# Where the up projection's four combinations of x are formed, and how many column pairs go the plain way

## The chip, the cores and the metric

The kernel runs on one core of a Trainium2 chip. The metric is the device time of one execution in microseconds (us). TensorE does the matmuls (PE in the profile, its weight loads PEld), VectorE is DVE, ScalarE is ACT, GpSimd is POOL, and SyncE (SP) issues most DMAs. All data is fp32; a matmul operand is split into a high and a low fp32r part ("hi" and "lo", hi + lo = the value), so that every product takes three matmuls.

## The reference, cut to what matters

One decoder layer: a hybrid mixer, a cross-attention, and the gated MLP below, with an RMSNorm around each. The change sits where the cross-attention's output becomes the MLP's input.

```
y = memory_cross_attention(rmsnorm(h, g[2]), rmsnorm(mem, mem_norm_g), w_q, w_kv, w_o)
h = h + rmsnorm(y, g[3])
x3 = rmsnorm(h, g[4])                              # (1024 tokens, 1024 columns)
u = causal_dwconv(x3 @ w_up, conv_w) + conv_b      # w_up: 1024 x 5632
a, b = split(u, 2)                                 # 2816 columns each
y = (silu(a) * b) @ w_down
```

## The kernel before, in words

**The cross-attention's output.** A loop over eight token tiles of 128 tokens, `t` = 0 to 7. In each, `token_mm` makes y for the tile in two PSUM banks (48 matmuls of 128x512), `post_norm` normalises it and adds the residual (L1005 to L1012), and L1103 to L1106 form `hr`, the normalised input of the MLP. Eight PE transposes of `hr` (L230, into two PSUM banks `tp_x3...`) and a split (ACT L232 writes hi, DVE L233 writes lo) make the transposed tile; it is put on the list `pend` and emitted behind the y of the next tile. Below, "token t" is this loop's tile, and `tp_x` of token t its transposes.

**x3** lies in SBUF as eight tiles [128, 4, 512]: token half (0 or 1) by part (hi, lo) by half of the 1024 columns. B11 and B21 are the two column halves of the first token half, B12 and B22 those of the second.

**The up projection** goes over 22 pairs of column blocks, `j` and `j + 22`. The first `PLAIN` pairs (three) go the plain way: for each block and token half 24 matmuls (`plain_mm`), so 96 a pair. The others go by `strassen_pair`, one level of the Strassen-Winograd scheme in seven half products of 12 matmuls, so 84 a pair. It needs the four combinations T1 = B12 - B11, T2 = B22 - T1, T3 = B22 - B12, T4 = B21 - T2, each as hi and lo tiles, and seven weight operands (A11, A12, A22, S1 to S4), which `up_operands` makes from the two raw weight blocks: four sums on POOL (L1151), seven splits on ACT (L1156) and DVE (L1157).

**The combinations** are made by `x_combinations`, in eight slices of 64 tokens: POOL adds hi and lo of the four B (L1198), DVE subtracts (L1201), ACT and DVE split the four results (L1203, L1204). Per slice 4 POOL, 8 DVE and 4 ACT instructions of 128x256. Four slices are written between the plain pairs 0 and 1, four behind pair 1.

**Order.** A scheduler fixes every engine's instruction order when the kernel is built; each engine then runs its own list in order. PSUM is split into tags: `mm` (5 banks) and `g` (3 banks) up to the end of the plain pairs, then `set_psum(b=8)` makes eight banks for the Strassen pairs, which come free when the old ones have been read out (`plain_out`, L1216). The pool `ap_` (`a_tile`) has nine buffers of 8 KB a partition (a tile of x3 or T, or the pair of tiles `ua`, fills one); the raw weight blocks have two buffers.

Of the kernel before, what the change touches and what calls it, by code (L numbers as in the profile page):

```python
# [7 lines left out]
F32 = mybir.dt.float32  # L8
F32R = mybir.dt.float32r
I32 = mybir.dt.int32  # L10
AF = mybir.ActivationFunctionType
ALU = mybir.AluOpType
# [4 lines left out]
P = 128  # L17
T = 1024
# [4 lines left out]
NC = 8  # L23
NFF = 22
# [38 lines left out]
    return [(n, int(e[len(n):])) for n, e in zip(names, text.split())]  # L63


PLAIN = 3


@with_exitstack
def hybrid_layer(  # L70
# [4 lines left out]
    nc = tc.nc  # L75
# [23 lines left out]
    h1_d = dram.tile([NC, P, D], F32, name="h1_d")  # L99
    h2_d = dram.tile([NC, P, D], F32, name="h2_d")  # L100
    mid_d = dram.tile([NFF, P, T], F32, name="mid_d")

    const = ctx.enter_context(pool("const"))
    wpool = ctx.enter_context(pool("wpool"))
# [13 lines left out]
    def psum(tag, name):  # L118
        p, tags = psum_pool[0]
        return p.tile([P, 512], F32, tag=tag, name=name, bufs=tags[tag])  # L120
# [69 lines left out]
        plan(f"wa{k}", a_d[k], gain=par[:, O_G2 + k:O_G2 + k + 1], where=(WX, W)[k // 4])  # L190
    for k in range(KT):
        plan(f"wv{k}", vw_d[k], where=(WX, W)[k // 4])
    for j in (0, NFF, 1, 1 + NFF, 2, 2 + NFF):
        plan(f"up{j}", w_up[j])

    def rsqrt(a, n, name):
# [25 lines left out]
        dve.tensor_scalar(a, ssq, 1.0 / d, EPS, op0=ALU.mult, op1=ALU.add)  # L222
        return rsqrt(a, n, name)

    def transpose_split(src, hi, lo, name):
        for q in range(2):
            tp = psum("g", f"tp_{name}_{q}")
            for i in range(4):
                k = 4 * q + i
                pe.transpose(out=tp[:, i * P:(i + 1) * P], in_=src[:, k * P:(k + 1) * P], identity=ident)  # L230
            v = tp.rearrange("p (k t) -> p k t", k=4)
            act.activation(hi(q), v, AF.Copy)  # L232
            dve.tensor_tensor(lo(q), v, hi(q), op=ALU.subtract)  # L233
# [752 lines left out]
    def a_tile(shape, name, dtype=F32R):  # L986
        return ap_.tile(shape, dtype, tag="a", name=name, bufs=9)
# [92 lines left out]
    for n in range(2):  # L1080
        g = wpool.tile([P, 512], F32, tag="st", name=f"g4{n}", bufs=2)
        sync.dma_start(out=g, in_=gains[4:5, HS[n]].to_broadcast([P, 512]))
        g4.append(g)
    x3 = [[[], []], [[], []]]
    for t in range(NC):
        hf = t // 4
        hr = wk(f"hr{t}")
        sync.dma_start(out=hr, in_=h1_d[t])
        if t == NC - 1:
            flush()  # L1090
        o = token_mm(pT[t], "wv", f"y{t}", t in ENDS)
        flush()
        if t % 4 == 0:
            for i in range(2):
                for q in range(2):
                    nm = f"x3_{hf}_{i}_{q}"
                    x3[hf][i].append(x8.tile([P, 4, 512], F32R, tag="x8", name=nm, bufs=4) if hf == 0
                                     else a_tile([P, 4, 512], nm))
        y = wk(f"h2{t}")
        post_norm(o, g3, y, hr, sqrt_r)  # L1100
        nc.scalar.dma_start(out=h2_d[t], in_=y)
        ss = small(1, "ss4")
        act.activation(hr, y, AF.Square, accum_out=ss)  # L1103
        r = sqrt_r(ss, 1, "r4")
        for n in range(2):
            dve.scalar_tensor_tensor(out=hr[:, HS[n]], in0=y[:, HS[n]], scalar=r, in1=g4[n],  # L1106
                                     op0=ALU.mult, op1=ALU.mult)
        s = slice((t % 4) * P, (t % 4 + 1) * P)
        pend.append(lambda hr=hr, hf=hf, s=s, t=t: transpose_split(
            hr, lambda k: x3[hf][0][k][:, :, s], lambda k: x3[hf][1][k][:, :, s], f"x3{t}"))  # L1110

# [50 lines left out]
            c = slice(k * P, (k + 1) * P)  # L1164
            mm3(o, w[0][:, c], w[1][:, c], xx[0][:, k], xx[1][:, k], start and k == 0, k == 3, not start)

    def strassen_pair(j, W_, ua, ub):
        b = [psum("b", f"st{j}_{n}") for n in range(4)]
        p1 = wpool.tile([P, 512], F32, tag="st", name=f"p{j}", bufs=2)
        u3 = gbp.tile([P, 512], F32, tag="gb", name=f"u3_{j}", bufs=1)  # L1170
        half_product(b[0], W_["A11"], X["B11"], True)
        act.activation(p1, b[0], AF.Copy)
        half_product(b[1], W_["S2"], X["T2"], True)
        dve.tensor_tensor(p1, b[1], p1, op=ALU.add)
        half_product(b[2], W_["S1"], X["T1"], True)
        dve.tensor_tensor(u3, b[2], p1, op=ALU.add)
        half_product(b[3], W_["S3"], X["T3"], True)
        dve.tensor_tensor(ub[:, 0, HS[1]], b[3], u3, op=ALU.add)
        half_product(b[0], W_["A12"], X["B21"], False)
        act.activation(ua[:, 0, HS[0]], b[0], AF.Copy)  # L1180
        half_product(b[2], W_["S4"], X["B22"], False)
        dve.tensor_tensor(ua[:, 0, HS[1]], b[2], p1, op=ALU.add)
        half_product(b[3], W_["A22"], X["T4"], False)
        dve.tensor_tensor(ub[:, 0, HS[0]], b[3], p1, op=ALU.add)
        a = conv3(j, ua)
        gate_mid(j, a, conv3(j + NFF, ub))

    X = {}

    def x_combinations(cs):  # L1190

        for c in cs:
            s = slice(c * 64, c * 64 + 64)
            xr = tp.tile([P, 4, 4, 64], F32, tag="tmp", name=f"xr{c}", bufs=2)
            raw = {}
            for i, n in enumerate(("B11", "B12", "B22", "B21")):
                raw[n] = xr[:, i]
                nc.gpsimd.tensor_tensor(raw[n], X[n][0][:, :, s], X[n][1][:, :, s], op=ALU.add)  # L1198
            for o, p, m in (("T1", "B12", "B11"), ("T3", "B22", "B12"), ("T2", "B22", "T1"), ("T4", "B21", "T2")):
                raw[o] = raw[{"T1": "B11", "T3": "B12", "T2": "B22", "T4": "B21"}[o]]  # L1200
                dve.tensor_tensor(raw[o], raw[p], raw[m], op=ALU.subtract)  # L1201
            for n in ("T2", "T1", "T3", "T4"):
                act.activation(X[n][0][:, :, s], raw[n], AF.Copy)  # L1203
                dve.tensor_tensor(X[n][1][:, :, s], raw[n], X[n][0][:, :, s], op=ALU.subtract)  # L1204

    def plain_mm(jj, i):
        os_[jj, i] = psum("mm", f"up{jj}_{i}")
        up_half(jj, os_[jj, i], i)
# [12 lines left out]
    for jj in (0, NFF, 1):  # L1221
# [2 lines left out]
    wx_es.close()  # L1224
    up_es = ExitStack()
    tp = up_es.enter_context(pool("tp"))
    tt = lambda n, i: (a_tile([P, 4, 512], f"xT{n}{i}") if n in (1, 2) else
                       tp.tile([P, 4, 512], F32R, tag="t", name=f"xT{n}{i}", bufs=4))
    for jj in (0, NFF):
        plain_mm(jj, 1)  # L1230
    plain_out(0)
    for n, (hf, q) in {"B11": (0, 0), "B21": (0, 1), "B12": (1, 0), "B22": (1, 1)}.items():
        X[n] = (x3[hf][0][q], x3[hf][1][q])
    X.update({f"T{n}": (tt(n, 0), tt(n, 1)) for n in (2, 1, 3, 4)})
    x_combinations(range(4))
    plain_mm(1, 1)
    for i in range(2):
        plain_mm(1 + NFF, i)
    plain_out(1)
    x_combinations(range(4, 8))  # L1240
    for jj in (2, 2 + NFF):
        for i in range(2):
            plain_mm(jj, i)
    plain_out(2)
    ops = {PLAIN: up_operands(PLAIN)}
    set_psum(b=8)
    for j in range(PLAIN, NFF):
        if j + 1 < NFF:
            ops[j + 1] = up_operands(j + 1)
        strassen_pair(j, ops.pop(j), a_tile([P, 2, T], f"ua{j}", F32),  # L1250
                      a_tile([P, 2, T], f"ua{j + NFF}", F32) if j % 2 else
                      tp.tile([P, 2, T], F32, tag="ua", name=f"ua{j + NFF}", bufs=1))
    up_es.close()
    ap_es.close()
    x8_es.close()
# [227 lines left out]
```

## Time and profile before

| what | us |
|---|---|
| median of 3 runs (lowest, highest) | 1495.16 (1494.82, 1496.19) |
| the profiled execution: its own time | 1496.32 |
| its span (first to last instruction) | 1494.5 |
| PE busy in the span | 1434.6 (96%) |
| DVE, ACT, POOL busy | 1161.3, 695.3, 169.5 |

A busy share is an average over stages. The row of granted clock (PEclk) is TensorE's clock as a share of full speed: 1.00 is 2.4 GHz, 0.50 is 1.2 GHz. Times below are counted from the start of the span. The DMA queues in the page are two hardware queues (issued by SP and by ACT) and two for instructions; no DMA of this kernel is issued by POOL.

### The profile page before, as it was taken

To read this page: it belongs to the slowest core of one execution; us is meant where nothing else is said; L and a number is where in the kernel's file an instruction comes from. 1 tells how busy PE (TensorE), PEld (TensorE's weight loads), DVE (VectorE), ACT (ScalarE), POOL (GpSimd) and SP (SyncE) were. 2 spreads that over 40 slices of the span, in tenths; PEclk is the share of its full clock that TensorE was granted. 3 is DMA by queue.
4 is the path that set the end of the run, shared out by engine and by line. 5 is a ranking of instruction groups with operands and counts; after the bars stand their busy time and mean duration, and the time that the engine had idled before them with its cause. 6 is when DMAs were issued, how large, how long until landed. Compare 5 with 4: busy or idle time off the path is not lost.

```text
span 1494.5 us, 19452 instructions
## 1 busy us (share of the span) xinstructions
PE 1434.6 (96%) x7099; PEld 1186.8 (79%) x7099; DVE 1161.3 (78%) x1993; ACT 695.3 (47%) x1326; POOL 169.5 (11%) x118
## 2 busy tenths in 40 slices
PE   6999999998999899999999989999999999999996
PEld 6878888887897778788788867888888887788875
DVE  6699999993567778743556777888888887869997
ACT  6526464633556545433434443444444444554442
POOL 0000000000000000000000643333333330000000
PEclk9999999999999999999999999999999999999998
DMA  7533233339756775400523112222222225985472
GB/s 243 166 96 100 71 109 82 106 103 290 218 173 206 240 225 184 141 29 0 169 100 123 46 43 71 77 78 85 85 85 79 77 85 203 319 301 197 140 254 107
DMA packets 118560, 205.74 MB, mean 138 GB/s; under 512 B 17184, under 2 KB 58816, under 8 KB 118464
## 3 DMA queue, kind: packets, MB, share of 16 engines
q1 hardware_dynamic: 95488, 155.99, 33.4%
q10 hardware_dynamic: 22976, 48.51, 8.7%
q8 instruction: 56, 0.92, 0.3%
q14 instruction: 40, 0.33, 0.1%
HBM read 153.58 MB, written 50.87 MB: 137 GB/s over the span
## 4 chain that ended last, share of the span: by engine, by line
PE 49%; DVE 6%; DMA 3%; issue 2%; ACT 2%; POOL 1%; DVEq 0%; SPq 0%; ACTq 0%; POOLq 0%
PE st L236 8%; PE st L238 8%; PE st L237 8%; PE M L237 3%; PE M L238 3%; PE M L236 3%; PE y L237 2%; PE y L238 2%; PE y L236 2%; PE sc L236 1%; PE sc L237 1%; PE sc L238 1%; PE wo L237 1%; PE wo L238 1%; PE wo L236 1%
## 5 line engine op out<-in xcount | busy, mean ns | idle before, releaser
L238 PE MATMUL pj<-xT,w_in 128*128 128x512 f32 x384 | 150.3, 391 | 1.2 <-DVE w_in L133 1.2
L352 DVE SCALAR_TENSOR_TENSOR ca<-sg,par,ca 128x1023 f32<-128x1023 f32 (+18 forms) x120 | 150.1, 1267 | 1.1
L236 PE MATMUL pj<-xT,w_in 128*128 128x512 f32 x384 | 150.8, 393 | 0.1
L237 PE MATMUL pj<-xT,w_in 128*128 128x512 f32 x384 | 149.9, 390 | 0.0
L237 PE MATMUL M<-wM 128*128 128x512 f32 x308 | 121.1, 393 | 4.6 <-DVE wM L1317 2.7
L1127 DVE SCALAR_TENSOR_TENSOR ua<-ua,par 128x1023 f32<-128x1023 f32 x88 | 115.6, 1315 | 9.7 <-ACT ua L1125 7.0
L236 PE MATMUL M<-wM 128*128 128x512 f32 x308 | 118.9, 392 | 4.4 <-ACT wM L132 3.5
L238 PE MATMUL M<-wM 128*128 128x512 f32 x308 | 120.8, 392 | 0.0
L236 PE MATMUL st<-xT,wst 128*128 128x512 f32 x304 | 118.7, 391 | 0.0
L238 PE MATMUL st<-xT,wst 128*128 128x512 f32 x304 | 118.4, 390 | 0.0
L237 PE MATMUL st<-xT,wst 128*128 128x512 f32 x304 | 118.2, 389 | 0.0
L236 PE MATMUL st<-x,wst 128*128 128x512 f32 x228 | 93.9, 412 | 9.2 <-ACT ua L1216 5.7
L1198 POOL TENSOR_TENSOR xr<-x,x 128x256 f32<-128x256 f32 x32 | 32.4, 1045 | 579.4 <-DVE hr L1106 562.2
L132 ACT ACTIVATE wM<-rbM 128x1024 fp32r<-128x1024 f32 x55 | 58.0, 1062 | 75.1 <-PE M L238 53.7
L238 PE MATMUL st<-x,wst 128*128 128x512 f32 x228 | 91.5, 401 | 0.0
L237 PE MATMUL st<-x,wst 128*128 128x512 f32 x228 | 91.3, 400 | 0.0
L1157 DVE TENSOR_TENSOR wst<-sums,wst 128x512 fp32r<-128x512 f32 x76 | 60.7, 818 | 35.0 <-ACT wst L1156 35.0
L1156 ACT ACTIVATE wst<-sums 128x512 fp32r<-128x512 f32 x76 | 43.8, 621 | 90.0 <-POOL sums L1151 90.0
L238 PEld LDWEIGHTS pj<-xT,w_in 128*128 128x128 f32 x384 | 72.1, 188 | 16.2 <-DVE w_in L133 1.5
L236 PEld LDWEIGHTS pj<-xT,w_in 128*128 128x128 f32 x384 | 72.1, 188 | 14.8 <-ACT w_in L132 0.3
L237 PEld LDWEIGHTS pj<-xT,w_in 128*128 128x128 f32 x384 | 72.2, 188 | 14.5
L133 DVE TENSOR_TENSOR wM<-rbM,wM 128x1024 fp32r<-128x1024 f32 x55 | 67.0, 1226 | 8.4 <-ACT wM L132 8.4
(376 smaller groups left out, 3654.7 us busy)
## 6 DMA issues: line engine op xcount, KB each, us to landing
rbM<-in_w_down SPq DMA_DIRECT2D x132, 256.0 KB, 4.0
raw_up<-in_w_up SPq DMA_DIRECT2D x44, 512.0 KB, 3.6
raw_in<-in_w_in SPq DMA_DIRECT2D x24, 512.0 KB, 3.7
mid_d<-ua ACTq DMA_DIRECT2D x22, 512.0 KB, 2.6
ma<-mid_d SPq DMA_DIRECT2D x44, 256.0 KB, 5.4
raw_kv<-in_w_kv SPq DMA_DIRECT2D x16, 512.0 KB, 4.4
h_d<-h ACTq DMA_DIRECT2D x16, 512.0 KB, 2.7
xr<-in_x ACTq DMA_DIRECT2D x8, 512.0 KB, 4.4
```

Source lines behind the costliest of these rows:

```text
L132: act.activation(w[:, 0], raw, AF.Copy)
L133: dve.tensor_tensor(w[:, 1], raw, w[:, 0], op=ALU.subtract)
L236: pe.matmul(o, lhsT=wh, rhs=xh, start=start, stop=False, skip_group_check=onto)
L237: pe.matmul(o, lhsT=wh, rhs=xl, start=False, stop=False, skip_group_check=onto)
L238: pe.matmul(o, lhsT=wl, rhs=xh, start=False, stop=stop, skip_group_check=onto)
L352: dve.scalar_tensor_tensor(out=ca[:, d:], in0=sg[:, :T - d], scalar=par[:, wb + 30 - d:wb + 31 - d], in1=ca[:, d:], op0=ALU.mult, op1=ALU.add)
L1127: dve.scalar_tensor_tensor(out=a[:, d:], in0=u[:, :T - d], scalar=fw(2 - d), in1=a[:, d:], op0=ALU.mult, op1=ALU.add)
L1156: act.activation(w[:, i, 0], op[s], AF.Copy)
L1157: dve.tensor_tensor(w[:, i, 1], op[s], w[:, i, 0], op=ALU.subtract)
L1198: nc.gpsimd.tensor_tensor(raw[n], X[n][0][:, :, s], X[n][1][:, :, s], op=ALU.add)
```

## The change

`x_combinations` goes, with its 32 POOL, 64 DVE and 32 ACT instructions. In its place `x3_tile` takes over the split of a transposed tile and, for tokens 4 to 7 (the second token half, when the first is there), also forms the four combinations of the tile's 128 tokens: B12 and B22 are read straight from the transposes' two PSUM banks, B11 and B21 as hi and lo from `x3`. That is six DVE subtractions or additions of 128x512 and one ACT copy a token. Those of tokens 4 to 6 are written by POOL to a DRAM tile `xt_d`, four DMAs of 256 KB a token in pieces of 512 bytes; those of token 7 stay in SBUF.

Later, between the plain pairs, `x_combination(i)` loads what tokens 4 to 6 left of one combination from `xt_d` into the place of its lo tile by a DMA of SP (768 KB in pieces of 1536 bytes), and ACT and DVE split it in two instructions each: 128x1536 for the loaded part, 128x512 for the part in SBUF. `PLAIN` is 2: pair 2 now goes by Strassen, with three banks of tag `g` and one of `mm` for its sums, before `set_psum(b=8)`. T3 and T4 take the buffers of `ap_` that T1 and T2 had.

```
-PLAIN = 3
+PLAIN = 2
...
+    xt_d = dram.tile([4, P, 4, 512], F32, name="xt_d")
...
-    for j in (0, NFF, 1, 1 + NFF, 2, 2 + NFF):
+    for j in (0, NFF, 1, 1 + NFF):
         plan(f"up{j}", w_up[j])
...
+    TN = (2, 1, 3, 4)
+    xt_last = []
+
+    def x3_tile(hr, hf, s, t):
+        tps = []
+        transpose_split(hr, lambda k: x3[hf][0][k][:, :, s], lambda k: x3[hf][1][k][:, :, s], f"x3{t}", tps)
+        if hf == 0:
+            return
+        xt = a_tile([P, 4, 512], f"xt{t}", F32)
+        v = [xt[:, i].rearrange("p (k t) -> p k t", k=4) for i in range(4)]
+        b12, b22 = (tp.rearrange("p (k t) -> p k t", k=4) for tp in tps)
+        sub = lambda o, a, b: dve.tensor_tensor(o, a, b, op=ALU.subtract)
+        act.activation(v[2], b12, AF.Copy)
+        sub(v[1], b12, x3[0][0][0][:, :, s])
+        sub(v[1], v[1], x3[0][1][0][:, :, s])
+        sub(v[0], b22, v[1])
+        sub(v[2], b22, v[2])
+        sub(v[3], x3[0][0][1][:, :, s], v[0])
+        dve.tensor_tensor(v[3], v[3], x3[0][1][1][:, :, s], op=ALU.add)
+        if t == NC - 1:
+            xt_last.extend(v)
+            return
+        for i in range(4):
+            nc.gpsimd.dma_start(out=xt_d[i][:, :, s], in_=v[i])
...
-        pend.append(lambda hr=hr, hf=hf, s=s, t=t: transpose_split(
-            hr, lambda k: x3[hf][0][k][:, :, s], lambda k: x3[hf][1][k][:, :, s], f"x3{t}"))
+        pend.append(lambda hr=hr, hf=hf, s=s, t=t: x3_tile(hr, hf, s, t))
...
-    def strassen_pair(j, W_, ua, ub):
-        b = [psum("b", f"st{j}_{n}") for n in range(4)]
+    def strassen_pair(j, W_, ua, ub, tags="bbbb"):
+        b = [psum({"m": "mm"}.get(tag, tag), f"st{j}_{n}") for n, tag in enumerate(tags)]
...
+    def x_combination(i):
+
+        hi, lo = X[f"T{TN[i]}"]
+        n = 3 * P
+        raw = lo[:, :, 0:n].bitcast(F32)
+        sync.dma_start(out=raw, in_=xt_d[i][:, :, 0:n])
+        for r, s in ((raw, slice(0, n)), (xt_last[i], slice(n, n + P))):
+            act.activation(hi[:, :, s], r, AF.Copy)
+            dve.tensor_tensor(lo[:, :, s], r, hi[:, :, s], op=ALU.subtract)
...
     for jj in (0, NFF):
         plain_mm(jj, 1)
+    x_combination(0)
     plain_out(0)
-    x_combinations(range(4))
+    x_combination(1)
     plain_mm(1, 1)
+    x_combination(2)
     for i in range(2):
         plain_mm(1 + NFF, i)
+    x_combination(3)
     plain_out(1)
-    x_combinations(range(4, 8))
-    for jj in (2, 2 + NFF):
-        for i in range(2):
-            plain_mm(jj, i)
-    plain_out(2)
```

**PE, between the y of token 6 and the y of token 7.** `y_1_7374` (before) and `y_1_7387` (after) are the last sums of token 6, `y_0_7483` and `y_0_7520` with `y_1_7521` those of token 7, `tp_x_0` and `tp_x_1` the transposes of token 5's `hr`. Before:

```order
L237 MATMUL y_1_7374<-w_wv_6787,pT_6653 128x512
L238 MATMUL y_1_7374<-w_wv_6787,pT_6653 128x512
L230 MATMUL tp_x_0_7423<-ident,hr_7275 128x128 x4
L230 MATMUL tp_x_1_7430<-ident,hr_7275 128x128 x4
L236 MATMUL y_0_7483<-w_wv_6752,pT_6838 128x512
```

With the change, the same transposes, eleven matmuls into token 7's y:

```order
L239 MATMUL y_1_7521<-w_wv_6758,pT_6839 128x512
L240 MATMUL y_1_7521<-w_wv_6758,pT_6839 128x512
L233 MATMUL tp_x_0_7436<-ident,hr_7276 128x128 x4
L241 MATMUL y_1_7521<-w_wv_6758,pT_6839 128x512
L233 MATMUL tp_x_1_7443<-ident,hr_7276 128x128 x4
L239 MATMUL y_0_7520<-w_wv_6763,pT_6839 128x512
```

They stand between two matmuls of one sum now; a late `hr` stops the y of token 7 there.

**DVE, behind the transposes of token 5.** `x_1_1_...` is the lo part of the transposed tile, `h_...` the residual of token 6, `xt_7450` the new tile of combinations. Before:

```order
L233 TENSOR_TENSOR x_1_1_0_7243<-tp_x_0_7423,x_1_0_0_7241 128x4x128
L233 TENSOR_TENSOR x_1_1_1_7244<-tp_x_1_7430,x_1_0_1_7242 128x4x128
L215 RECIPROCAL pn_y<-pn_y 128x1
L216 SCALAR_TENSOR_TENSOR pn_u<-pn_y,pn_a 128x1
L217 SCALAR_TENSOR_TENSOR pn_y<-pn_u,pn_y 128x1
L1010 SCALAR_TENSOR_TENSOR h_7437<-y_0_7373,pn_y,gb_6740 128x512
L1010 SCALAR_TENSOR_TENSOR h_7437<-y_1_7374,pn_y,gb_6740 128x512
L1012 TENSOR_TENSOR h_7437<-h_7437,hr_7371 128x1024
```

With the change:

```order
L236 TENSOR_TENSOR x_1_1_0_7244<-tp_x_0_7436,x_1_0_0_7242 128x4x128
L236 TENSOR_TENSOR x_1_1_1_7245<-tp_x_1_7443,x_1_0_1_7243 128x4x128
L1013 SCALAR_TENSOR_TENSOR h_7462<-y_1_7387,pn_y,gb_6741 128x512
L1101 TENSOR_TENSOR xt_7450<-tp_x_0_7436,x_0_0_0_6854 128x512
L1015 TENSOR_TENSOR h_7462<-h_7462,hr_7384 128x1024
L1101 TENSOR_TENSOR xt_7450<-xt_7450,x_0_1_0_6856 128x512
L1101 TENSOR_TENSOR xt_7450<-tp_x_1_7443,xt_7450 128x512 x2
L1101 TENSOR_TENSOR xt_7450<-x_0_0_1_6855,xt_7450 128x512
L134 TENSOR_TENSOR w_up_7603<-raw_up_7601,w_up_7603 128x1024
L1108 TENSOR_TENSOR xt_7450<-xt_7450,x_0_1_1_6857 128x512
L215 TENSOR_SCALAR r_a<-ss_7480 128x1
```

The six new instructions stand among those that lead to token 6's `hr` (its `r_a` is the last row), and ahead of them.

**POOL, its list from the last memset on.** `xt_...` are the tiles of tokens 4, 5 and 6, `sums_...` the weight sums of the first Strassen pair. Before, 32 additions `xr` stood here; with the change:

```order
L1113 DMA xt_d<-xt_7342 512x1x128 x4
L1113 DMA xt_d<-xt_7450 512x1x128 x4
L1113 DMA xt_d<-xt_7508 512x1x128 x4
L1180 ISA
L1180 TENSOR_TENSOR sums_0_7909<-raw_up_7907 128x512
L1180 TENSOR_TENSOR sums_1_7910<-raw_up_7905,raw_up_7907 128x512
L1180 TENSOR_TENSOR sums_0_7909<-sums_0_7909,raw_up_7905 128x512
L1180 TENSOR_TENSOR sums_1_7910<-raw_up_7905,sums_0_7909 128x512
```

The first pair's sums now stand behind twelve DMA issues in place of 32 additions.

## Rows read from the trace of the kernel before

**Rows 1.** The waits of PE in the whole span: times waited, longest.

```profile
PE st L236 <- ACT ua L1216: 5.7, 1, 5.7
PE st L236 <- DVE u L1176: 3.5, 1, 3.5
```

**Rows 2.** Stretches: length, busy us (instructions) of PE, PEld, DVE, ACT, POOL; granted clock; DMA.

```profile
798.35:810.10 11.75, 11.75 (x57) 9.86 (x56) 7.66 (x17) 5.95 (x12) 0.00 (x0) 1.00 0.25 89
810.10:828.90 18.80, 18.55 (x88) 14.89 (x88) 10.23 (x21) 6.57 (x14) 5.48 (x8) 1.00 0.41 132
828.90:878.80 49.90, 49.90 (x216) 40.38 (x216) 44.13 (x74) 25.22 (x48) 27.23 (x26) 1.00 0.12 40
878.80:884.51 5.71, 0.00 (x0) 0.00 (x0) 3.78 (x8) 3.26 (x8) 4.13 (x3) 0.78 0.07 28
884.51:888.91 4.40, 4.40 (x11) 3.46 (x11) 3.94 (x4) 3.23 (x5) 2.87 (x2) 0.51 0.16 22
904.07:909.34 5.27, 5.27 (x12) 4.12 (x13) 1.89 (x3) 0.00 (x0) 0.00 (x0) 0.50 0.01 3
912.09:931.53 19.44, 19.44 (x85) 15.69 (x84) 15.83 (x18) 8.51 (x12) 7.18 (x4) 1.00 0.24 80
```

**Rows 3.** Timeline of POOL and ACT about 880 us: start, length, instruction, [idle before].

```profile
878.46 2.71 POOL L1151 TENSOR_TENSOR sums<-raw_up 128x512 f32<-128x512 f32 x1 [5.51 <-DVE xT L1204]
...
883.40 1.06 ACT L1216 ACTIVATE ua<-up 128x512 f32<-128x512 f32 x2
```

**Rows 4.** DVE by line, 828.9 to 878.8 us: busy, mean ns, idle before.

```profile
L1201 DVE TENSOR_TENSOR xr<-xr 128x256 f32<-128x256 f32 x30 | 17.0, 578 | 5.8 <-POOL xr L1198 5.3
L1127 DVE SCALAR_TENSOR_TENSOR ua<-ua,par 128x1023 f32<-128x1023 f32 (+1 forms) x8 | 12.1, 1514 | 0.0
L1204 DVE TENSOR_TENSOR xT<-xr,xT 128x256 fp32r<-128x256 f32 x29 | 11.4, 438 | 0.0
```

**Rows 5.** Timeline of DVE behind the y of token 5.

```profile
787.29 0.16 DVE L1007 TENSOR_TENSOR pn_s<-pn_ss 128x1 f32<-128x1 f32 x1 [2.32 <-ACT h L1005]
...
789.50 1.41 DVE L1010 SCALAR_TENSOR_TENSOR h<-y,pn_y,gb 128x512 f32<-128x512 f32 x2
790.95 1.22 DVE L1012 TENSOR_TENSOR h<-h,hr 128x1024 f32<-128x1024 f32 x1
...
795.22 1.42 DVE L1106 SCALAR_TENSOR_TENSOR hr<-h,r_y,g 128x512 f32<-128x512 f32 x2
```

**Rows 6.** The instructions on the transposes' banks, 700 to 830 us: shortest/median/longest ns.

```profile
L233 DVE TENSOR_TENSOR x<-tp_x,x x16: 680/691/692, 744.1 to 829.5; 128x512 fp32r<-128x512 f32 x16
```

**Rows 7.** Timeline of PE at the transposes of token 7.

```profile
827.61 1.04 PE L230 MATMUL tp_x<-ident,hr 128*128 128x128 f32 x8
828.90 0.98 PE L236 MATMUL up<-x,w_up 128*128 128x512 f32 x3 [0.25 <-ACT x L232]
```

**Rows 8.** Timeline of PE: two other waits; then the stretches around them, as in rows 2.

```profile
522.11 0.50 PE L237 MATMUL wo<-w_wo,mxt 128*128 128x512 f32 x1 [1.40 <-DVE w_wo L133]
...
373.05 0.39 PE L236 MATMUL a<-kvw,w_q 128*128 128x256 f32 x1 [2.37 <-ACT w_q L132]
...
521.00:526.00 5.00, 3.68 (x18) 2.81 (x19) 2.41 (x3) 1.25 (x2) 0.00 (x0) 1.00 0.52 174
...
372.00:377.00 5.00, 3.95 (x19) 3.40 (x20) 3.18 (x4) 2.54 (x3) 0.00 (x0) 0.66 1.04 383
```

**Rows 9.** POOL's dearest instruction, and what one DMA issue costs ACT's queue.

```profile
L1151 POOL TENSOR_TENSOR sums<-raw_up x19: 1603/1916/2715, 878.5 to 1228.5; 128x512 f32<-128x512 f32 x19
...
792.20 0.33 ACTq L1101 DMA_DIRECT2D h_d<-h  x1
```

**Rows 10.** DMA issues: count, KB each, median us from issue to landing.

```profile
raw_up<-in_w_up SPq DMA_DIRECT2D x44, 512.0 KB, 3.6
...
h_d<-h ACTq DMA_DIRECT2D x16, 512.0 KB, 2.7
...
raw_eg<-gc_d SPq DMA_DIRECT2D x4, 512.0 KB, 7.1
```

More of the change, by code (lines that the diff above doesn't have):

```diff
@@ L223, in rms_r, with transpose_split @@
         return rsqrt(a, n, name)
-    def transpose_split(src, hi, lo, name):
+    def transpose_split(src, hi, lo, name, tps=None):
         for q in range(2):
             tp = psum("g", f"tp_{name}_{q}")
+            if tps is not None:
+                tps.append(tp)
             for i in range(4):
@@ L1188, in hybrid_layer @@
     X = {}
[L1190 to L1204, printed above, removed]
+    def x_combination(i):
[6 more added lines that the diff above has]
+            dve.tensor_tensor(lo[:, :, s], r, hi[:, :, s], op=ALU.subtract)
     def plain_mm(jj, i):
@@ L1226, in hybrid_layer @@
     tp = up_es.enter_context(pool("tp"))
-    tt = lambda n, i: (a_tile([P, 4, 512], f"xT{n}{i}") if n in (1, 2) else
+    tt = lambda n, i: (a_tile([P, 4, 512], f"xT{n}{i}") if n in (3, 4) else
                        tp.tile([P, 4, 512], F32R, tag="t", name=f"xT{n}{i}", bufs=4))
+    for n, (hf, q) in {"B11": (0, 0), "B21": (0, 1), "B12": (1, 0), "B22": (1, 1)}.items():
+        X[n] = (x3[hf][0][q], x3[hf][1][q])
+    X.update({f"T{n}": (tt(n, 0), tt(n, 1)) for n in TN})
     for jj in (0, NFF):
         plain_mm(jj, 1)
+    x_combination(0)
     plain_out(0)
-    for n, (hf, q) in {"B11": (0, 0), "B21": (0, 1), "B12": (1, 0), "B22": (1, 1)}.items():
-        X[n] = (x3[hf][0][q], x3[hf][1][q])
-    X.update({f"T{n}": (tt(n, 0), tt(n, 1)) for n in (2, 1, 3, 4)})
-    x_combinations(range(4))
+    x_combination(1)
     plain_mm(1, 1)
+    x_combination(2)
     for i in range(2):
         plain_mm(1 + NFF, i)
+    x_combination(3)
     plain_out(1)
-    x_combinations(range(4, 8))
-    for jj in (2, 2 + NFF):
-        for i in range(2):
-            plain_mm(jj, i)
-    plain_out(2)
     ops = {PLAIN: up_operands(PLAIN)}
-    set_psum(b=8)
     for j in range(PLAIN, NFF):
@@ L1251, in hybrid_layer @@
                       a_tile([P, 2, T], f"ua{j + NFF}", F32) if j % 2 else
-                      tp.tile([P, 2, T], F32, tag="ua", name=f"ua{j + NFF}", bufs=1))
+                      tp.tile([P, 2, T], F32, tag="ua", name=f"ua{j + NFF}", bufs=1),
+                      "gggm" if j == PLAIN else "bbbb")
+        if j == PLAIN:
+            set_psum(b=8)
     up_es.close()
```

## The prediction

> **What bounds the kernel now.** PE is busy for 96% of the span, so time is won only where PE waits or runs slowly, or where it gets fewer matmuls. I read PE's waits over the whole span first. Two of the longer ones stand next to each other at the first Strassen pair: 5.7 us before its first matmul and 3.5 us inside it [rows 1]. Then I cut the neighbourhood into stretches [rows 2]. What the reader is to see there, in order: the three first half-blocks of the up projection end in the transposes of token 7; from 828.90 to 878.80 the other nine plain half-blocks run without a gap, 216 matmuls in 49.90, 0.231 each; then PE does nothing for 5.71; then 11 matmuls take 4.40 and, behind the second wait, 12 take 5.27, at a granted clock of 0.51 and 0.50, that is 1.2 GHz in place of 2.4. From 912.09 a Strassen pair takes 19.44 at clock 1.00, and it stays so. Pair 3, the first Strassen pair, took 912.09 - 884.51 = 27.58, so it lost 8.14: 3.5 of it a wait, the rest mostly half clock.
>
> Why PE waits at 878.8 is seen in the timeline [rows 3]: POOL starts on the weight sums of the first Strassen pair only at 878.46, when DVE has given back the slices of x; ACT, in order, reads out the last plain banks only at 883.40, behind splits of T and of those sums. In the 49.90 us before, DVE was busy for 44.13 [rows 2], 28.4 of them with the combinations alone [rows 4]. So the combinations decide when the Strassen pairs can start.
>
> **The change, step by step.** I name E5, E6, E7 the ends of the y matmuls of tokens 5, 6 and 7; E6 is 798.35 and E7 810.10 [rows 2].
>
> *Fewer matmuls.* Pair 2 needs 84 in place of 96: 96 x 0.231 = 22.18 becomes 19.44 [rows 2]: -2.7.
>
> *The wait of 5.71.* PE reaches the first Strassen pair after 5 plain half-blocks (120 matmuls, 27.7) in place of 9 (216). What must be done by then: DVE has, from the transposes of token 7 to the sixth split of the first pair's weights, 2 splits and 5 + 1 combinations of 128x512 at 0.69 [rows 6], three parts of T of 128x1536 at 1.5 x 1.22 = 1.83 [rows 5] (an estimate by length), three of 128x512, four convolutions at 1.51 at most [rows 4], one 128x1024 product at 1.22, six weight splits at 0.69: 5.5 + 5.5 + 2.1 + 6.0 + 1.2 + 4.1 = 24.4 of the 27.7. PE's opening product needs only the list up to the first weight split, A11: 24.4 less the product and five splits, 19.8. Transposes 1.2 later than before (below) start it at 830.1, so A11 is ready at 850, or 851 with the loads of T (below), and PE is there at 857.9. That leaves 7 us to spare, and the wait goes: -5.7. The cover is those 27.7 us of plain matmuls; if it were gone, the wait would be back one for one.
>
> *Pair 3's stall and the slow clock.* The second wait came because DVE and ACT were still busy with the late splits; the next pair's weights are asked for when A12 of the first pair is split, about 853, and used at 877, as far ahead as in the undisturbed pairs. So two pairs at 19.44 follow: -8.1. What is late next is T4, used last in the pair (from 875); it is split at about 857.
>
> *More DVE work beside y.* In tokens 5, 6 and 7 six instructions of 0.69 join DVE's list: +4.1 a token. Token 6 has 11.75 us and DVE is busy for 7.66 of them; up to 828.9 it is busy for 10.23 of 18.80 [rows 2]. Two tokens' worth fits, but the chain to `hr` grows longer. Before, it took from 787.29 to 796.64 [rows 5], and its transposes came at about 798.4. Now ACT's list has the root of token 5's norm behind the square of token 6's last y, so `hr` of token 5 is whole at E6 + 3.7, its first half at E6 + 3.0; PE wants it after eleven matmuls, at E6 + 2.5: a wait of 0.5. Token 6 comes out even. Token 7's `hr` has token 6's six instructions and, as before, the splits of the first plain weights ahead of it; I get E7 + 18.0 and + 18.7 for its halves, where PE comes to it at E7 + 17.8 (before: 827.61, that is + 17.5 [rows 7]). Together with the matmul fragments around the transposes I take +1.2; nothing lost is the one end, 1.5 for each of three transposes, +4.5, the other. Such waits leave the clock alone: one of 1.40 stood in a stretch granted 1.00, one of 2.37 in a stretch granted 0.66 [rows 8].
>
> *The twelve stores from POOL.* The trace has no DMA issued by POOL. From below, the issue costs what it costs ACT, 0.33; from above, POOL's dearest instruction, 2.72; I take that row's shortest, 1.6, since POOL must work on 512 pieces [rows 9]. POOL is idle there, and at either end the four stores of a token are done within the 11.75 to the next. The combinations of token 6 end at about E6 + 24 = 822; with 4 x 1.6 and a landing like that of a store of 512 KB, 2.7 [rows 10], all are in DRAM by 831, those of T2 by 827. Cost: 0. A rule of the Trainium skill speaks against POOL as issuer (*SBUF — State Buffer*, the box on the "DVE blocks DMA" trap): POOL cannot write a DMA's descriptors while a DVE instruction holds the port pair that they share, and a DMA of 620 ns then took about 3100. Taking its 3.1 a store, the last one would be in DRAM by about 839 and the sum the same, with 3 us to spare in place of 7. No run here shows it; it raises the chance of the slow rival below, no more.
>
> *The four loads of T.* 768 KB each; by length 1.5 x 3.6 = 5.4 from a weight block, 1.5 x 7.1 = 10.7 from the slowest of such loads [rows 10]. I take 5.4, whole rows being nearest, and one behind the other: T2 at 831, T3 837, T1 842, T4 848. They stand in SP's queue ahead of the weights of pair 3, which wait for a buffer until 853 anyway. ACT wants T1, the third, at 839; its list slips by 3, which DVE's list feels as the 1 us above. At 10.7 T1 would land at 858 and A11 be ready at 867: a wait of 9 and some 2 us of slow clock, +11.
>
> *POOL's, DVE's and ACT's work for the old combinations* lay beside PE and is worth nothing beyond the waits above.
>
> **The sum** against the profiled execution's span: 1494.5 - 2.7 - 5.7 - 8.1 + 1.2 = 1479.2. The execution's own time was 1.8 above the span, so 1481.0, and 1.16 above the median of the runs shown: **1479.8**. (A measurement of this kernel can tell about 0.2%, 3 us, from no change.)
>
> **The rivals.**
> *Partly.* The stall moves and does not vanish: T loads near the dear end, or DVE's list too full beside y, or the first pair's operands a few us late. For it: DVE has 24.4 us of work in 27.7, and its `hr` waits of ACT. Against it: 7 us to spare. A wait of 3 to 9 with 2.4 of slow clock (11 matmuls at 0.40 in place of 0.231 lose 1.9, 12 at 0.44 lose 2.5 [rows 2]) gives 1483 to 1491.
> *Slower.* POOL's stores are dear. T1's load waits in SP's queue behind T3's, and that for the third store of token 6. The first 4 stores start at about 795; from about 3.5 us a store they are late for PE, above 4 each token's stores queue behind the last one's and the third of token 6 ends at 795 + 11 s. Every us of it beyond 835.7 is a wait of PE, with 2.4 of slow clock. At 4.9 us a store the gain is gone; at 6 the third ends at 861, 25.3 late: 1479.8 + 25.3 + 2.4 = 1507.5. For it: 512 pieces a store, and the unknown issuer. Against it: both rows that bound the price lie under 3.
> *Nothing.* The bank wait stays for a reason of its own (the Strassen banks of pair 3 lie on banks that the last plain pair must still empty), and only the 2.7 are won, less the 1.2: 1493.7. Against it: pair 2 now opens on three banks of the transposes and a spare one, read out 20 us before.
>
> **How the numbers follow.** My forecast's own range is 1477.5 to 1482.5 (no loss beside y gives 1478.6; three transposes waited for 1.5 each 1483.1), chance 0.62. Partly: 0.23. Slower: 0.10. Nothing: 0.05. To hold 8 in 10 the range takes in the partial cases up to the dear end of the loads, 1491, and a little under the lower bound: 1477 to 1491. Faster by over 0.2% (below 1492.2): 0.62 + 0.23 = 0.85; within it: 0.05; slower: 0.10.
>
> **What would show it.** Right, if the profile has no wait of PE over 1 us between 798 and 900, a granted clock of 1.00 throughout that stretch, 5 plain half-blocks of 24 matmuls behind the transposes of token 7 and two Strassen pairs of about 19.4 behind them. Waits of 0.3 to 1 at the transposes of tokens 5 and 7 would bear out the cost beside y. The stores are priced by POOL's queue and by when T's loads land: by 850 or not. I would be wrong if ACT or DVE stood waiting for a load of T near 850 with PE idle behind them, if POOL's sums came later than 845, or if a half-clock stretch showed up beside the y of tokens 5 to 7.

## The result, and the profile after

| | before, us | with the change, us | ratio (95% interval) |
|---|---|---|---|
| first measurement | 1495.62 (1494.82 to 1496.19, 4 runs) | 1477.01 (1476.20 to 1481.40, 4 runs) | 0.9884 (0.9867 to 0.9901) |
| repeated (below) | 1496.79 (1494.22 to 1502.00, 17 runs) | 1481.38 (1479.87 to 1485.93, 5 runs) | 0.9897 (0.9877 to 0.9917) |

The changed kernel is 18.6 us faster in the first measurement and 15.4 in the second. The forecast was 1479.8, and 15.3 us by its sum.

The page of the changed kernel, first line of its engines:

```profile
PE 1428.7 (97%) x7087; PEld 1183.2 (80%) x7087; DVE 1162.9 (79%) x1971; ACT 694.7 (47%) x1309; POOL 150.5 (10%) x102
```

The span went from 1494.5 to 1475.1, PE's busy time by only 5.9 of those 19.4: most of what was won is time in which PE stood still, 9.2 us of it in the two waits of [rows 1]. PE's waits of the changed kernel between 735 and 960 us, from the transposes of the first tokens into the Strassen pairs (what waited, for whom, us in total, times, longest); it is the whole list, where before two waits of 5.7 and 3.5 stood beside this one [rows 1]:

```profile
PE up L239 <- ACT x L235: 0.2, 1, 0.2
```

The same neighbourhood cut into stretches (from and to, length, busy time and count of each engine, granted clock, DMA share, GB/s), the counterpart of [rows 2]:

```profile
806.96:825.89 18.93, 18.93 (x90) 15.02 (x88) 15.37 (x32) 7.72 (x16) 3.59 (x5) 1.00 0.85 252
825.89:853.99 28.10, 27.85 (x121) 22.55 (x121) 26.38 (x27) 20.50 (x29) 5.87 (x4) 1.00 0.37 134
853.99:873.40 19.41, 19.41 (x86) 15.89 (x85) 14.68 (x18) 9.82 (x14) 5.53 (x4) 1.00 0.17 56
873.40:892.82 19.42, 19.42 (x86) 15.75 (x85) 16.88 (x18) 8.61 (x12) 6.50 (x4) 1.00 0.26 84
```

Five plain half-blocks lie behind the transposes of token 7, in 28.10 with the last transposes; then two Strassen pairs of 19.4 each, all at clock 1.00. The stall of 5.71 and the pair of 27.58 are gone.

How close it was is read from DVE's timeline of the changed kernel (start, duration, line, operation, out<-in):

```profile
846.18 0.67 DVE L1186 TENSOR_TENSOR wst<-raw_up,wst 128x512 fp32r<-128x512 f32 x1
...
852.23 1.76 DVE L1227 TENSOR_TENSOR xT<-xT,xT 128x1536 fp32r<-128x1536 f32 x1 [1.23 <-ACT xT L1226]
853.91 0.68 DVE L1227 TENSOR_TENSOR xT<-xt,xT 128x512 fp32r<-128x512 f32 x1
```

and from PE's:

```profile
853.76 0.39 PE L241 MATMUL up<-x,w_up 128*128 128x512 f32 x1
853.99 0.40 PE L239 MATMUL st<-x,wst 128*128 128x512 f32 x1
```

A11, the first operand, is whole at 846.85; PE takes it at 853.99. That is 7.1 us to spare where the prediction had 7. T4's last part is whole at 854.6 and used some 16 us later.

**Where the time came from.** Two points that every version has, the first transpose of the MLP's input and the first matmul of the down projection (`M`), take the parts ahead of the change and behind it out of the comparison. From the rows of each tile's instructions (count, ns min/median/max, first to last start), before, in a second profile of that kernel:

```profile
L236 PE MATMUL st<-x,wst x228: 389/396/796, 884.3 to 1258.3; 128*128 128x512 f32 x114
L230 PE MATMUL tp_x<-ident,hr x64: 270/272/275, 742.6 to 828.1; 128*128 128x128 f32 x64
L236 PE MATMUL M<-wM x308: 388/389/796, 1261.7 to 1484.0; 128*128 128x512 f32 x154
```

and with the change, in its first profile:

```profile
L239 PE MATMUL st<-x,wst x240: 389/397/501, 854.0 to 1239.0; 128*128 128x512 f32 x120
L233 PE MATMUL tp_x<-ident,hr x64: 270/272/300, 739.6 to 825.6; 128*128 128x128 f32 x64
L239 PE MATMUL M<-wM x308: 387/389/795, 1242.7 to 1465.0; 128*128 128x512 f32 x154
```

| stretch | before | after | difference |
|---|---|---|---|
| first to last transpose | 85.5 | 86.0 | +0.5 |
| last transpose to first Strassen matmul | 56.2 | 28.4 | -27.8 |
| Strassen pairs (19, then 20), to the first `M` | 377.4 | 388.7 | +11.3 |
| sum: first transpose to first `M` | 519.1 | 503.1 | -16.0 |

So the change is worth 16.0 us in its own stretch. The rest of the 19.4 lies ahead of it: the first transpose stands at 739.6 in this profile, at 742.6 and 742.9 in the two of before. The experiments come back to that. The stretch of 519.1 or 503.1 is called **the stretch** below.

### The profile page after: what moved, and what is told of

Read it like the earlier page. It is cut to its first block, busy times and chain, and to the rows that moved or that the text cites. A ratio compares the mean times of both kernels' runs of the same rounds, so it can differ in the third digit from the quotient of the medians.

```text
span 1475.1 us, 19398 instructions
## 1 busy us (share of the span) xinstructions
PE 1428.7 (97%) x7087; PEld 1183.2 (80%) x7087; DVE 1162.9 (79%) x1971; ACT 694.7 (47%) x1309; POOL 150.5 (10%) x102
## 4 chain that ended last, share of the span: by engine, by line
PE 80%; DVE 7%; DMA 7%; ACT 2%; issue 2%; SPq 0%; DVEq 0%; ACTq 0%
PE st L239 9%; PE st L241 9%; PE st L240 8%; PE pj L241 6%; PE pj L239 6%; PE pj L240 6%; PE M L240 4%; PE M L241 3%; PE M L239 3%; PE y L240 2%; PE y L241 2%; PE y L239 2%; PE sc L240 1%; PE sc L241 1%; PE sc L239 1%
## 5 line engine op out<-in xcount | busy, mean ns | idle before, releaser
L239 PE MATMUL st<-xT,wst 128*128 128x512 f32 x320 | 125.0, 391 | 0.0
L241 PE MATMUL st<-xT,wst 128*128 128x512 f32 x320 | 124.7, 390 | 0.0
L240 PE MATMUL st<-xT,wst 128*128 128x512 f32 x320 | 124.4, 389 | 0.0
L1156 DVE SCALAR_TENSOR_TENSOR ua<-ua,par 128x1023 f32<-128x1023 f32 x88 | 112.5, 1281 | 10.3 <-ACT ua L1154 7.4
L239 PE MATMUL st<-x,wst 128*128 128x512 f32 x240 | 96.8, 403 | 0.0
L241 PE MATMUL st<-x,wst 128*128 128x512 f32 x240 | 94.7, 394 | 0.0
L240 PE MATMUL st<-x,wst 128*128 128x512 f32 x240 | 94.2, 393 | 0.0
L240 PEld LDWEIGHTS M<-wM 128*128 128x128 f32 x308 | 58.4, 190 | 18.2 <-DVE wM L1340 3.6
```

The lines of the kernel that those rows point to most:

```text
L239: pe.matmul(o, lhsT=wh, rhs=xh, start=start, stop=False, skip_group_check=onto)
L240: pe.matmul(o, lhsT=wh, rhs=xl, start=False, stop=False, skip_group_check=onto)
L241: pe.matmul(o, lhsT=wl, rhs=xh, start=False, stop=stop, skip_group_check=onto)
L1156: dve.scalar_tensor_tensor(out=a[:, d:], in0=u[:, :T - d], scalar=fw(2 - d), in1=a[:, d:], op0=ALU.mult, op1=ALU.add)
```

## The experiments

Twelve runs follow: the two kernels once more, and ten versions. The table has each one's median beside the kernel before on the same chip, and from its one profile the first transpose and the stretch; the text takes them one by one.

| version | median, us | before there, us | ratio | first transpose | the stretch | against the change |
|---|---|---|---|---|---|---|
| before once more | 1496.4 (1 run) | 1497.5 | | 742.6 | 519.1 | +16.0 |
| changed kernel once more | 1481.4 | 1496.8 | 0.9897 | 746.5 | 502.9 | -0.2 |
| early combinations, three plain pairs | 1483.7 | 1496.8 | 0.9912 | 746.5 | 505.3 | +2.2 |
| late combinations, two plain pairs | 1507.8 | 1496.8 | 1.0064 | 742.8 | 528.3 | +25.2 |
| early combinations, one plain pair | 1493.0 | 1496.8 | 0.9976 | 743.9 | 517.5 | +14.4 |
| banks as before | 1481.6 | 1498.7 | 0.9889 | 745.7 | 503.2 | +0.1 |
| DVE's work beside y doubled | 1485.6 | 1497.5 | 0.9927 | 746.0 | 508.9 | +5.8 |
| stores from SP | 1479.1 | 1497.5 | 0.9884 | 746.3 | 502.7 | -0.4 |
| stores from ACT | 1486.4 | 1498.7 | 0.9920 | 744.4 | 505.9 | +2.8 |
| loads of T made twice | 1483.1 | 1498.7 | 0.9900 | 742.5 | 504.4 | +1.3 |
| two small DMAs ahead of each store | 1515.3 | 1498.7 | 1.0115 | 740.4 | 531.6 | +28.5 |
| seven small DMAs ahead of each store | 1643.0 | 1497.5 | 1.0980 | 744.4 | 665.3 | +162.2 |

**The theory** is the prediction's: the late combinations kept DVE and POOL busy, so the first Strassen pair's operands were late, and ACT's reading of the banks behind their splits with them; plain pairs are the cover for that work, and twelve matmuls are saved by the way. **The rivals**: the saved matmuls or the other banks count, or something ahead of the change.

**1. Both kernels once more.**

> The changed kernel once more, unchanged, as a yardstick. Two readings of the 3.2 us by which its first profile was already ahead of the one of before when the transposes of the cross-attention's output began (739.6 against 742.9, instructions up to there in the same order on every engine). Chance of the execution: the start of these transposes moves by 1 us or more from profile to profile, and the median of this kernel falls between 1476 and 1481. Systematic (the new DRAM tile, or what it moves in memory): it stays within 0.5 us of 739.6, and the median within 1 us of 1477.0.

> The kernel before once more, for its profile alone. If the 3.2 us ahead of the change are chance, the transposes of the cross-attention's output begin 1 us or more away from 742.9, and PE's wait of 2.4 us for a split of w_q near 372 is shorter or gone; if they belong to the kernel, both stay within 0.5 us. Time 1495.6 within 2.

The first transpose of the changed kernel moved from 739.6 to 746.5 with nothing changed, the median to 1481.4. The stretch stayed: 502.9. So the 3.2 us by which the first profile was ahead are no gift of the change. For the kernel before, the second profile stood at 742.6, within the 0.5 us that spoke for a property of the kernel, though its wait for `w_q` was 1.5 in place of 2.4. Over the eleven profiles with early combinations the first transpose stands at 739.6 to 746.5, over the three with late ones at 742.6 to 742.9. The instructions up to there are in the same order on every engine, apart from a few matmuls of the mixer on PE, which change places between the two profiles of the kernel before as well. What spreads them (short waits between 350 and 640 us that differ from profile to profile) was not tried, nor whether the narrow spread of the three is more than luck.

**2. One more plain pair.**

> Combinations made early, as in the change, but three plain pairs again. My theory (the early combinations remove the wait and the slow pair, the third Strassen pair only saves twelve matmuls): no wait at the first Strassen pair, clock 1.00, and 22.18 - 19.44 = 2.7 us over the changed kernel, 1479.7 if that is at 1477.0. Rival (much of the gain is the pair that goes the other way, or its three early banks): half of the 18.6 us lost or more, 1486 and above.

```
-PLAIN = 2
+PLAIN = 3
...
     plain_out(1)
+    for jj in (2, 2 + NFF):
+        for i in range(2):
+            plain_mm(jj, i)
+    plain_out(2)
```

2.3 us slower than the changed kernel by the medians of the same chip, 2.2 by the stretch, where 2.7 was said; no wait of PE at the first Strassen pair, clock 1.00. With early combinations and the old number of plain pairs 13 of the 15 us are there already: the saved matmuls are the small part.

**3. One plain pair fewer, without the early combinations.**

> The kernel before with two plain pairs in place of three, and the combinations made late as they were. My theory (DVE's and POOL's late combinations decide when a Strassen pair can start, the plain pairs only cover them): the weight sums of the first Strassen pair come some 7 us earlier than 878.5, since pair 2 needs no convolutions and product from DVE any more, but PE is there 22.2 us earlier, so it waits about 20 us in place of 5.7; the first pair takes 27.6 again, and the next one 19.4: it ends about 12 us later than before, 1507 (1503 to 1514). Rival (the saved matmuls count by themselves): 1495.6 - 2.7 = 1492.9.

```
-PLAIN = 3
+PLAIN = 2
...
-    for jj in (2, 2 + NFF):
-        for i in range(2):
-            plain_mm(jj, i)
-    plain_out(2)
```

Slower than before by 11 us, 1507.8 where 1507 was said. PE's waits of this kernel around the first pairs:

```profile
PE st L236 <- ACT p L1172: 9.3, 1, 9.3
PE st L236 <- ACT ua L1216: 8.1, 1, 8.1
PE st L236 <- DVE u L1176: 1.9, 1, 1.9
```

and what stood behind them on POOL:

```profile
871.88 2.24 POOL L1151 TENSOR_TENSOR sums<-raw_up 128x512 f32<-128x512 f32 x1 [0.70 <-DVE xT L1204]
```

POOL's sums begin 6.6 us earlier than before [rows 3], where 7 was said, but PE is there 22 us earlier. It waits 19.3 in all, less than was said (about 20 before the pair and 3.5 inside it), and in other portions. The first operand, A11, comes early; PE waits 8.1 for the last plain banks, which ACT reads out at 864.0, behind splits of T. Behind the first half product it stops for 9.3, until ACT reads the first bank out at 877.7, behind splits of POOL's late sums. That is the theory's case, and the rival's 1492.9 is far off: fewer plain matmuls are a loss where the combinations are late.

**4. One plain pair, with the early combinations.**

> The changed kernel with one plain pair in place of two. My theory (five plain half-blocks behind the transposes are the cover; in the changed kernel's profile the second part of the first pair's first weight operand is written at 846, the last part of T4 at 855): PE is there 22.2 us earlier, at about 832, DVE has some 7 us less to do, so PE waits 7 to 14 us, with 2.4 of slow clock behind it and 2 to 5 inside the pair; less the 2.7 of twelve matmuls that is 9 to 16 us over the changed kernel, 1486 to 1493. Rival (there was far more slack than that, and DVE's list shortens when the plain pair goes): 2.7 under it, 1474.3.

```
-PLAIN = 2
+PLAIN = 1
...
-    plain_mm(1, 1)
     x_combination(2)
-    for i in range(2):
-        plain_mm(1 + NFF, i)
     x_combination(3)
-    plain_out(1)
```

(The third half-block ahead of the last transposes goes with it.) 11.6 slower than the changed kernel by the medians, inside the 9 to 16, so the cover theory holds for the size. The place was not the one expected. PE's rows with a wait:

```profile
827.88 1.94 PE L233 MATMUL tp_x<-ident,hr 128*128 128x128 f32 x8 [4.27 <-DVE hr L1136]
848.69 0.50 PE L240 MATMUL st<-xT,wst 128*128 128x512 f32 x1 [1.05 <-DVE xT L1227]
853.05 0.79 PE L239 MATMUL st<-x,wst 128*128 128x512 f32 x1 [3.86 <-ACT p L1201]
884.66 0.50 PE L239 MATMUL st<-x,wst 128*128 128x512 f32 x1 [2.30 <-DVE u L1205]
```

The third half-block had been the cover for `hr` of token 7, and without it PE waits 4.27 there. The first operand is not late at all (DVE splits A11 at 817.6, beside y); the pair loses its time inside: first for the third of the combinations, whose last part DVE writes at 847.95, then for ACT, which reads the first bank out only at 852.4, behind its parts of T, of the plain pair and of the weights. The next pair waits 2.30 more. So of one, two and three plain pairs, two are the best number here.

**5. The banks.**

> The changed kernel with the first Strassen pair's four sums in the eight banks that all later pairs use, as before, in place of three banks of the transposes and a spare one. My theory (the wait of 5.7 us before the first Strassen pair was one for late operands, and for an ACT that was late behind them): ACT reads out the last plain banks within 0.6 us of their last matmul now, so PE waits 2 us at most and the time stays within 2 us of the changed kernel. Rival (the wait belongs to the banks): 4 to 6 us of wait before the first Strassen pair, and 2 more of slow clock.

```
+        if j == PLAIN:
+            set_psum(b=8)
         strassen_pair(j, ops.pop(j), ...
-                      "gggm" if j == PLAIN else "bbbb")
-        if j == PLAIN:
-            set_psum(b=8)
```

The stretch is 503.2, and there is no wait before the first Strassen pair: in the changed kernel the other banks are worth nothing. The wait of before was named after ACT's reading of the banks [rows 1]. Rows of DVE and ACT in the kernel before show what stood behind it:

```profile
855.67 0.68 DVE L1157 TENSOR_TENSOR wst<-raw_up,wst 128x512 fp32r<-128x512 f32 x1
...
881.21 0.63 ACT L1156 ACTIVATE wst<-sums 128x512 fp32r<-128x512 f32 x1 [2.04 <-POOL sums L1151]
882.55 0.63 ACT L1156 ACTIVATE wst<-sums 128x512 fp32r<-128x512 f32 x1 [0.41 <-POOL sums L1151]
...
883.87 0.68 DVE L1157 TENSOR_TENSOR wst<-sums,wst 128x512 fp32r<-128x512 f32 x1
```

A11 is whole there at 856.35, 22 us before PE comes to it, so the first operand was not what was late. ACT read the last plain banks out at 883.40 [rows 3] because it had waited for POOL's sums and split them first. With free banks PE could have run the first half product, 12 matmuls or 2.8 us, and would then have waited for the second operand, S2, whose low part DVE writes at 883.87; by this estimate other banks alone could have given back at most half of the 5.7. The kernel before with other banks was not run.

**6. DVE's work beside y.**

> The changed kernel with six more DVE subtractions of 128x512 a token beside the cross-attention's output (three of the combinations' are made three times), 4.1 us a token for tokens 4 to 7. The prediction counted 1.2 us for the six that are there, in waits of PE for the transposes of tokens 5 and 7; the profile shows none. If there was just enough room, the six more cost what was forecast for the first or more, 1.5 to 8 us, in waits at the transposes; if token 7's list is the tight one only (its operands have 3 to 7 us of slack), less than 2.

```
+        for _ in range(2):
+            sub(v[1], b12, x3[0][0][0][:, :, s])
+            sub(v[1], v[1], x3[0][1][0][:, :, s])
+            sub(v[0], b22, v[1])
         act.activation(v[2], b12, AF.Copy)
```

The stretch is 5.8 longer. There is one wait, for `hr` of token 7; tokens 5 and 6 have none:

```profile
835.57 1.94 PE L233 MATMUL tp_x<-ident,hr 128*128 128x128 f32 x8 [4.53 <-DVE hr L1140]
```

So the six instructions of the change just fit, and the next 4.1 us a token show at token 7 in full, with slow clock behind: from 835.57 to 840.80 the granted clock is 0.50, that is 1.2 GHz, and the transposes take 1.94 in place of 1.04 [rows 7].

**7. Who issues the stores.**

> The changed kernel with the twelve stores issued by SP in place of POOL. My theory (any queue will do, since POOL was idle and the stores had slack): within 1 us of the changed kernel. Rival (the issuer matters, because SP's queue carries the weights of the up projection, which the stores now stand ahead of, waiting for DVE): the first plain weights come late, a wait of PE of 1 to 5 us near 826 to 840.

> The changed kernel with the twelve stores issued by ACT in place of POOL. If any queue will do: within 2 us of the changed kernel, as with SP. Rival (ACT's list is in order and also carries the square and the root that make the next token's hr, so a store that waits for DVE's combination holds these up): waits of PE of 1 to 4 us at the transposes of tokens 5 to 7, as when DVE had six subtractions more.

```
-            nc.gpsimd.dma_start(out=xt_d[i][:, :, s], in_=v[i])
+            sync.dma_start(out=xt_d[i][:, :, s], in_=v[i])
```

(and `nc.scalar` for ACT). The issue of one store, the first row from the changed kernel:

```profile
L1113 POOL DMA_DIRECT2D xt_d<-xt x12: 709/723/903, 787.7 to 818.1; - x12
L1224 SPq DMA_DIRECT2D xT<-xt_d x4: 518/676/943, 820.1 to 822.3; - x4
```

from SP:

```profile
L1113 SPq DMA_DIRECT2D xt_d<-xt x12: 513/540/852, 794.1 to 824.5; - x12
```

and from ACT, whose timeline has the stores of token 5 ahead of the square that `hr` of token 6 needs:

```profile
808.09 1.95 ACTq L1113 DMA_DIRECT2D xt_d<-xt  x3
810.08 0.66 ACTq L1131 DMA_DIRECT2D h_d<-h  x1
811.75 0.52 ACTq L1113 DMA_DIRECT2D xt_d<-xt  x1
812.32 1.06 ACT L1133 ACTIVATE hr<-h 128x1024 f32<-128x1024 f32 x1 [3.38 <-DMA xt_d<-xt]
```

SP does as well as POOL (-0.4 by the stretch). From ACT it costs 2.8: the square stands idle for 3.38 behind the last of the four stores, which waits for DVE's combination, token 6's chain runs late, and PE waits 2.18 at the transposes of token 7. So it is not the price of an issue that counts (0.72, 0.54 and 0.52 us) but what stands behind it in the list.

**8. The loads of T made twice.**

> The changed kernel with each of the four loads of T made twice, the second over the first. The loads went side by side and had landed by 834; with the second ones behind them the last T is there at about 845 to 850. My theory (7 us of slack before the first weight operand, and T4 wanted last): at most 3 us over the changed kernel. Rival (loads one behind the other at 5.4 us each, as the prediction reckoned: eight of them end at 863, T1, wanted by ACT third, at 852 or later): PE waits 5 to 12 us.

```
+        for _ in range(2):
-        sync.dma_start(out=raw, in_=xt_d[i][:, :, 0:n])
+            sync.dma_start(out=raw, in_=xt_d[i][:, :, 0:n])
```

The eight issues last until 848:

```profile
822.99 24.93 SPq L1225 DMA_DIRECT2D xT<-xt_d  x8
```

and the last loaded part is split on ACT at 854.6, where the first Strassen matmul stands at 856.7. The stretch is 1.3 longer, with one wait of 1.05 inside the pair. The slack behind the loads is real: T4 may come as late as PE's arrival.

**9. Dearer stores.**

> The changed kernel with seven small DMAs more on POOL's queue ahead of each of the twelve stores (512 pieces of 16 bytes to a DRAM tile that nobody reads), to price the rival in which the stores are dear. The profile shows 0.72 us for the issue of one, so a store then costs about 5.8 us. By the prediction's formula the third store of token 6 ends at 795 + 11 x 5.8 = 859, 23 us later than PE can bear, and with 2.4 of slow clock the time is 1477 + 26 = 1503. If the issue of the small ones costs less, or the loads have more slack than that formula gives them, it stays nearer to 1477; if the small DMAs hold up the rest of the transfers, it goes beyond.

> The changed kernel with two small DMAs more on POOL's queue ahead of each of the twelve stores. With seven more, a store and its small ones took about 15.5 us of the queue in the long run, so a small one takes about 2.1 and a store with two of them about 4.9, where the prediction said the gain would be gone: its formula has the third store of token 6 end at 795 + 11 x 4.9 = 849, 13 us late, and with 2.4 of slow clock 1477 to 1481 become 1493 to 1497. If there is more slack behind the loads than the formula says, less: 1480 to 1490.

```
+    xt_e = dram.tile([3, 4, 7, P, 4, 4], F32, name="xt_e")
...
         for i in range(4):
+            for e in range(7):
+                nc.gpsimd.dma_start(out=xt_e[t - 4, i, e], in_=v[i][:, :, 0:4])
             nc.gpsimd.dma_start(out=xt_d[i][:, :, s], in_=v[i])
```

(2 in place of 7 in the other.) Both ended far beyond the forecasts of 1503 and 1493 to 1497: 1643.0 and 1515.3. The mechanism is the one that the first expectation named last: the small DMAs hold up the other transfers. In the one with two, T's loads are not what PE waits for first:

```profile
829.71 0.79 PE L240 MATMUL up<-x,w_up 128*128 128x512 f32 x1 [9.53 <-ACT w_up L134]
843.18 1.94 PE L234 MATMUL tp_x<-ident,hr 128*128 128x128 f32 x8 [4.71 <-DVE hr L1139]
```

The DMAs of that kernel from 790 to 900 us (KB each, median us to landing; 23 of the 24 small ones) and the stretch of that wait show why:

```profile
xt_d<-xt POOLq DMA_DIRECT2D x12, 256.0 KB, 13.7
raw_up<-in_w_up SPq DMA_DIRECT2D x6, 512.0 KB, 13.2
...
xt_e<-xt POOLq DMA_DIRECT2D x23, 8.0 KB, 13.3
```

```profile
820.20:829.71 9.51, 0.00 (x1) 0.01 (x1) 0.03 (x1) 1.11 (x2) 2.15 (x3) 0.77 1.01 151
```

The DMA engines are busy throughout at 151 GB/s, and a weight block lands after 13.2 us where it took 3.6 [rows 10]. From 790 to 850 us they are busy for the whole of the time at 108 GB/s, where the changed kernel has them busy for 0.56 of it at 179. The small stores hold up everything that goes through the same engines, the plain weights first. The experiment did not isolate the price of POOL's issue, which it was made for: its formula for late stores was neither borne out nor refuted.

No version beat the changed kernel by more than its own spread.

## Why the prediction was right

The mechanism is the predicted one, and the stretch shows its terms one by one.

- **Fewer matmuls, -2.7, and the wait, -5.7.** Together with the 22.2 us of a plain pair that moved behind, the forecast for the time from the last transpose to the first Strassen matmul was -27.9; it is -27.8. Experiment 2 priced the pair by itself at 2.2 to 2.3, a little under 2.7.
- **Pair 3's stall and half clock, -8.1.** The Strassen pairs grew by 11.3: one pair of 19.44 more, less 8.1.
- **Beside y, +1.2.** Measured +0.5, and without the waits that were to cause it: no row of PE waits at the transposes of tokens 5 to 7. The step that was off is the pessimistic end of `hr` for tokens 5 and 7. That it was near is shown by experiments 6 and 7, where 4 us of work more on DVE or ACT brought 4.5 and 2.2 us of wait at token 7. The sum was -15.3, the stretch gives -16.0, and the difference is this term.
- **The stores, 0.** They cost 0.72 us each, inside the bounds of 0.33 and 2.72 and under the 1.6 taken [rows 9]. The rule weighed there, that POOL cannot write descriptors while a DVE instruction holds the shared port pair (the Trainium skill, *SBUF — State Buffer*, the box on the "DVE blocks DMA" trap), does not show in these rows: the dearest of the twelve issues took 0.90, beside DVE subtractions of 0.69. DVE ran fp32 subtractions there and not the fp32 copy that the box names, so the rule as such is not refuted.
- **The loads, 5.4 each and one behind the other.** Wrong in the mechanism and harmless: the four were issued within 2.2 us and were under way together; they landed 6.9 to 11.5 us after their issue, all by 834. The 848 reckoned is 845 on this profile's clock, which runs 3 us ahead, so they were 11 us early. ACT's and DVE's lists, not the loads, set A11. That the time to spare is 7.1 as reckoned is partly luck: the sum charged 1 us for the loads and 6.0 for the four convolutions, which took 5.0, and nothing for DVE's slower instructions beside POOL, some 3 us (last section).
- **The rivals.** "Partly" and "Nothing" did not come: the banks are worth nothing in the changed kernel (experiment 5). The low end of "Partly", 1483, leaves out the 2.4 of slow clock that its sentence names. "Slower" did not come because its condition did not: an issue costs 0.72. What dear issues would do stays open, since experiment 9 slowed the DMA engines instead, and with them the weights and `hr`, before T's loads were late.

The first measurement's median lies 2.8 under the forecast and the repeat's 1.6 over it. The part ahead of the change moves by up to 7 us from profile to profile, so one profile of each kernel would have put 3 us more than it deserves down to the change.

## What to carry to other kernels

Matmuls that need nothing new are the cover for the operands of those that do: count what an earlier start of PE asks of the lists of the other engines before taking the cover away. Here the same edit, one plain pair fewer, lost 11 us with late operands, won 2 with early ones, and lost 12 when repeated. Compare two versions between two points that both have, around the change, and not by the spans alone; and ask of a DMA not only what its issue costs but what stands behind it in its queue, and on the DMA engines.

## What was not expected of the hardware

- DVE instructions with two inputs from SBUF took 1.7 us in place of 0.69 while POOL worked on the weight sums. From the timeline of the changed kernel, DVE:

```profile
828.32 1.68 DVE L1101 TENSOR_TENSOR xt<-xt,x 128x512 f32<-128x512 f32 x1
830.03 1.29 DVE L1101 TENSOR_TENSOR xt<-tp_x,xt 128x512 f32<-128x512 f32 x2
831.24 1.72 DVE L1101 TENSOR_TENSOR xt<-x,xt 128x512 f32<-128x512 f32 x1
832.88 1.78 DVE L1227 TENSOR_TENSOR xT<-xt,xT 128x512 fp32r<-128x512 f32 x1
```

and POOL:

```profile
828.16 1.28 POOL L1180 TENSOR_TENSOR sums<-raw_up 128x512 f32<-128x512 f32 x1 [9.32 <-ACT ua L1239]
829.41 1.74 POOL L1180 TENSOR_TENSOR sums<-raw_up,raw_up 128x512 f32<-128x512 f32 x1
831.11 1.30 POOL L1180 TENSOR_TENSOR sums<-sums,raw_up 128x512 f32<-128x512 f32 x1
832.48 1.63 POOL L1180 TENSOR_TENSOR sums<-raw_up,sums 128x512 f32<-128x512 f32 x1
```

The two of 830.03, with one input from PSUM, kept their 0.65 each. The Trainium skill (*SBUF — State Buffer*, "SBUF: two separate sides") says that a DVE operation with two SBUF inputs and a GpSimd operation that reads SBUF exclude each other on the port pair that they share; these rows agree. It lengthened DVE's list by some 3 us; the 7.1 us to spare are what was left.

- A DMA of 8 KB in 512 pieces of 16 bytes held the DMA engines for 0.6 to 1.4 us, one of 256 KB in 512 pieces for 0.86. The software queue of the changed kernel was busy for 0.7% of the span with twelve stores, which makes 0.86 us of all engines each. With 24 small ones more it was 2.9% of 1506.6, which makes 1.4 each; with 84 more 3.8% of 1641.6, which makes 0.6 each.
